# A count on VectorE in two steps: marks of half of the columns, then comparison of the other half with the marks added and summed

## The chip, the cores and the metric

The kernel runs on one core of one Trainium2 chip. The metric is the device time of one execution in microseconds; the kernel before took 3424.11 us as the median of three runs (3422.59 to 3427.55).

The core has five engines with one instruction queue each, and each queue is worked off in order: TensorE (PE in the rows, with its weight loads as PEld), VectorE (DVE), ScalarE (ACT), GpSimd (POOL) and SyncE (SP), which issues the DMAs here. They wait for each other by semaphores.

## The reference

One decoder block over a sequence of 2048 positions with 1024 features, in float32: a root-mean-square norm, one input projection, then a state-space branch and an attention branch side by side, merged with sigmoid gates, and a dense SwiGLU feed-forward layer (2816 wide).

The change lies in the attention branch. For each query an index score over all visible keys is formed, and only the 256 keys with the best scores take part in the attention:

```
rel    = relu(einsum('bqhd,bsd->bqhs', qi, ki))
iscore = einsum('bqhs,bqh->bqs', rel, wi * w_scale)
iscore = where(key_pos <= pos_q, iscore, -inf)
_, idx = top_k(iscore, 256)          # ties: the earlier key
logits = q . k[idx] * a_scale;  p = softmax(logits);  o = p . v[idx]
```

## The kernel before

**Tiles.** The 2048 queries are 16 tiles of 128, one query per partition. Tile i sees W = (i + 1) * 128 keys, so its scores are `S[i]`, a 128 x W tile of float32. Tiles 0 and 1 see no more than 256 keys and need no search.

**The key search (`topk`, from line 798).** For each query the 256th largest score is found bit by bit. A threshold `tr` is held for each query, and for each of 31 bits the kernel counts how many scores reach the threshold with that bit set; the next bit follows from the count (`un`, then `tr`, two very small VectorE instructions). The tiles are searched in four searches: tiles 2 and 3; 4 to 7; 8 to 11; 12 to 15. In each, the widest tiles are "wide": their counts are made by ScalarE with a sign function and a sum (`jka`). The narrow ones are counted by VectorE in `count` (line 849): tile 2 in the first search, tiles 4 and 5 in the second, 8 and 9 in the third, 12 and 13 in the fourth. The first count of every search is made on the float32 scores, wide tiles too. The next 15 bits of a narrow tile are counted on `H`, a copy of the upper halves of its scores as bfloat16 (threshold `tr`), the last 16 on `H` rewritten with the lower halves as uint16 (threshold `tf`); between the two stand the few wide instructions that rewrite `H` (`sgn`, `off`, `top`). At the end there is one more count on float32 scores for every tile (`gt`, line 951), and the marks of the selected keys are written out.

A count before is one VectorE instruction over all W columns: compare with the threshold, write the marks (0 or 1) to `jkd`, and sum them. In the trace it is a `TENSOR_SCALAR_CACHE_REDUCE` followed by a `DVE_READ_ACCUMULATOR`, which writes the sum out.

**What sets the order.** The whole program is written by one planner, `Pace` (line 42). It holds a clock for each engine, adds a planned cost for each instruction (`note`), and at each point takes the first of three streams (state-space branch, attention, dense layers) whose next step can start. A search step is taken as soon as VectorE is planned to be at most 7 us ahead of TensorE (`idle`, `AHEAD`). The costs there decide only the order; the engines then run at their own pace. So a cheaper count in the planner's eyes moves the work of all engines against the searches.

**What runs beside the searches.** The first and second search run beside the state-space branch and the gate projections (`gps`, `gw`), the third beside the dense layers of the first block of 512 queries (block 0), whose weights are still split into a high and a low part by GpSimd, ScalarE and VectorE (`ww<-raw`, `wd<-raw`), the fourth beside block 1 and the start of block 2. In a block TensorE writes to PSUM banks (`f`: three, and four more that the search leaves free), and VectorE empties them: `x<-f,x` adds a bank of the down projection, `g<-g,f` scales a gate, `t<-t,f` joins gate and up projection, after which ScalarE casts the result (`at<-t`) and VectorE subtracts (`at<-t,at`); only then can TensorE go on with the down projection (`f<-wd,at`).

Of the kernel before, what the change touches and what calls it, by code (L numbers as in the profile page):

```python
# [18 lines left out]
ALU = mybir.AluOpType  # L19
# [32 lines left out]
class Pace:  # L52
# [95 lines left out]
    def at(self, eng, *what):  # L148

        return lambda: self.when(eng, what) + (None,)  # L150
# [5 lines left out]
    def idle(self, eng, *what, on=None):  # L156

        return lambda: self.when(eng, what) + (on or eng,)
# [207 lines left out]
class Block:  # L366
# [431 lines left out]
    def topk(self, st, groups, KL):  # L798

        nc, at, idle = self.nc, self.pace.at, self.pace.idle  # L800
# [5 lines left out]
        def iscore(i, S, kis):  # L806
            W = (i + 1) * 128
            qi = qp.tile([128, IH, 128], F32R, name="qi")
            nc.sync.dma_start(qi.bitcast(F32), self.qi_d[i])
            for c in range(0, W, 512):  # L810
                n = min(512, W - c)
                m = min(512, (n + 255) // 256 * 256)
                for hp in range(IH // 2):
                    yield idle("PE", qi, kis, psp.free_at("tps"), on="DVE")
                    ps = psp.tile([128, 2, 512], F32, name="tps")
                    for h2 in range(2):
                        for p in range(2):
                            nc.tensor.matmul(ps[:, h2, :m], qi[:, hp * 2 + h2], kis[:, p, c:c + m],
                                             start=p == 0, stop=p == 1)
                    R = qp.tile([128, 2, 512], F32, name="R")  # L820
                    nc.scalar.activation(R[:, :, :n], ps[:, :, :n], AF.Relu)
                    for h2 in range(2):
                        w = self.wi[:, i, hp * 2 + h2:hp * 2 + h2 + 1]
                        if hp == 0 and h2 == 0:
                            nc.vector.tensor_scalar(S[:, c:c + n], R[:, 0, :n], w, None, op0=ALU.mult)
                        else:
                            nc.vector.scalar_tensor_tensor(S[:, c:c + n], R[:, h2, :n], w, S[:, c:c + n],
                                                           op0=ALU.mult, op1=ALU.add)
            dg = S[:, W - 128:W]
            nc.gpsimd.affine_select(dg, dg, pattern=[[-1, 128]], compare_op=ALU.is_ge, fill=LOW, base=0,  # L830
                                    channel_multiplier=1)
# [4 lines left out]
        S = {}  # L836
# [9 lines left out]
        self.spare_banks = 4  # L846
        jka, jkd = (qp.tile([128, L], BF16, name=n, tag="R") for n in ("jka", "jkd"))

        def count(x, i, t, c):

            nc.vector.tensor_scalar(jkd[:, :(i + 1) * 128], x, t, 0.0, op0=ALU.is_ge, op1=ALU.add, accum_out=c)

        def search(j, tiles, b, wide):

# [9 lines left out]
            for q, i in enumerate(tiles):  # L864
                yield idle("DVE")
                count(S[i], i, t[:, q:q + 1], cnt[:, q:q + 1])
# [8 lines left out]
            def missed(out, value, signs):  # L875

                if signs:
                    W = (tiles[0] + 1) * 128
                    nc.vector.tensor_scalar(out, cnt, float(W - 2 * TOPK + 1), float(value), op0=ALU.is_gt, op1=ALU.mult)
                else:  # L880
                    nc.vector.tensor_scalar(out, cnt, float(TOPK), float(value), op0=ALU.is_lt, op1=ALU.mult)

            for bit in range(30, -1, -1):
# [33 lines left out]
                for q, i in enumerate(tiles):  # L917
                    if wide:
                        nc.scalar.activation(jka[:, :(i + 1) * 128], S[i], AF.Sign, bias=t[:, q:q + 1], scale=-1.0,
                                             accum_out=cnt[:, q:q + 1])  # L920
                    else:
                        yield idle("DVE")
                        count(X[i], i, (tf if low else t)[:, q:q + 1], cnt[:, q:q + 1])
# [14 lines left out]
        for j, (tiles, b) in enumerate(states):  # L938
            n = len(tiles)
            tr = qp.tile([128, n], I32, name="trf")  # L940
            gt = qp.tile([128, n], F32, name="gt")
            fx = qp.tile([128, n], I32, name="fx")
            sg = qp.tile([128, n], I32, name="sg")
            sg2 = qp.tile([128, n], F32, name="sg2")
            ss = qp.tile([128, n], F32, name="ssum")
            nT = qp.tile([128, n], F32, name="nT")
            bf = b.bitcast(F32)
            yield idle("DVE")
            for q, i in enumerate(tiles):
                W = (i + 1) * 128  # L950
                nc.vector.tensor_scalar(jkd[:, :W], S[i], bf[:, q:q + 1], 0.0, op0=ALU.is_gt, op1=ALU.add,
                                        accum_out=gt[:, q:q + 1])
            nc.vector.tensor_scalar(fx, gt, float(TOPK), None, op0=ALU.is_ge)
            nc.vector.tensor_scalar(sg2, b, 0.0, None, op0=ALU.is_ge)
            nc.vector.tensor_scalar(sg, sg2, 2.0, -1.0, op0=ALU.mult, op1=ALU.add)
            nc.vector.tensor_tensor(tr, b, sg, op=ALU.add)
            nc.vector.copy_predicated(b, fx, tr)
            nc.vector.tensor_scalar(nT, bf, -1.0, None, op0=ALU.mult)

            todo = deque(enumerate(tiles))  # L960
            halves = deque()

            def sign():
                nonlocal order
                if todo:
                    q, i = todo.popleft()
                    W = (i + 1) * 128
                    sv, ev = (fin[:, order % 2, z, :W] for z in range(2))
                    order += 1
                    nc.scalar.activation(sv, S[i], AF.Sign, bias=nT[:, q:q + 1], scale=1.0,  # L970
                                         accum_out=ss[:, q:q + 1])
                    halves.append((q, i, W, sv, ev))
            yield idle("ACT", nT)
            sign()
            while halves:
                q, i, W, sv, ev = halves.popleft()
                yield idle("DVE", ss)
                sign()
                nc.vector.tensor_scalar(ev, sv, 0.0, None, op0=ALU.is_equal)
                nc.vector.tensor_tensor_scan(S[i], ones.to_broadcast([128, W]), ev, 0.0, op0=ALU.mult, op1=ALU.add)  # L980
                yield idle("DVE")
                r = qp.tile([128, 1], F32, name="r")
                r2 = qp.tile([128, 1], F32, name="r2")
                nc.vector.tensor_scalar(r2, gt[:, q:q + 1], -1.0, float(TOPK), op0=ALU.mult, op1=ALU.add)
                nc.vector.scalar_tensor_tensor(r, ss[:, q:q + 1], float(W - TOPK), gt[:, q:q + 1],
                                               op0=ALU.add, op1=ALU.subtract)
                nc.vector.tensor_scalar(r, r, -1.0, None, op0=ALU.mult)
                nc.vector.copy_predicated(r2, fx[:, q:q + 1], r)
                nc.vector.scalar_tensor_tensor(ev, S[i], r2, ev, op0=ALU.is_gt, op1=ALU.mult)
                yield idle("DVE")  # L990
                nc.vector.tensor_tensor(ev, ev, sv, op=ALU.subtract)
                nc.vector.tensor_scalar(ev, ev, 0.0, -BIG, op0=ALU.max, op1=ALU.mult)
                yield at("SP", ev)
                nc.sync.dma_start(self.bias_d[i], ev)
# [1008 lines left out]
```

## Time and profile before

| | |
|---|---|
| median of three runs | 3424.11 us |
| the profiled execution's own time | 3425.84 us |
| its span (first to last instruction) | 3424.1 us |
| TensorE busy | 3179.7 us, 93% |
| VectorE busy | 2150.5 us, 63% |
| ScalarE busy | 1262.8 us, 37% |
| GpSimd busy | 638.6 us, 19% |
| mean granted TensorE clock | 0.971 |

Busy times are sums over the whole span. The searches lie at about 388 to 475 us, 880 to 942, 1408 to 1640 and 2123 to 2390; what counts there is read from each stretch by itself. All instructions of the program have the same line in the profile (a recording helper), so they are told apart by the names of their tiles.

### The profile page before, as it was taken

Reading aid. Unit: us, or ns where it says so; the run is one execution under the profiler, and the core shown is the slowest. Engines: PE = TensorE matmul, PEld = TensorE weight load, DVE = VectorE, ACT = ScalarE, POOL = GpSimd, SP = SyncE. Lnnn points to the kernel's source line nnn. Section 1 sums busy time; section 2 is a strip of 40 time slices with the busy share of each in tenths; the row PEclk is TensorE's granted clock in tenths of the full one; section 3 lists DMA queues with packets and bytes.
Section 4 is the critical chain, followed back from the end, with each engine's and each line's share of the span. In section 5 each row is a group of like instructions: output and inputs, shape, how many; then the busy total and the mean of one; then the engine's idle time right before and its main releaser. Section 6 shows DMA issues by size and latency. Waiting matters only on the chain. (4 is left out here: it accounts for less than half of the span.)

```text
span 3424.1 us, 43974 instructions
## 1 busy us (share of the span) xinstructions
PE 3179.7 (93%) x16292; PEld 2684.6 (78%) x16292; DVE 2150.5 (63%) x4299; ACT 1262.8 (37%) x2192; POOL 638.6 (19%) x631
## 2 busy tenths in 40 slices
PE   6999989898978999987899999989899999999999
PEld 5889768677757887775788887768788888798887
DVE  5565686665886666889777667987766664322222
ACT  3141545454732444463024444761234342010000
POOL 3323676521222212343100000001000000000000
PEclk8999999999999999998999999989999999999999
DMA  4834433445368656566762334456453333755544
GB/s 134 250 114 117 127 106 108 157 121 156 108 222 289 225 179 226 198 239 249 262 225 112 140 108 171 165 209 227 183 187 131 115 110 141 302 207 200 205 165 183
DMA packets 321527, 605.68 MB, mean 177 GB/s; under 512 B 52896, under 2 KB 205216, under 8 KB 290592
## 3 DMA queue, kind: packets, MB, share of 16 engines
q1 hardware_dynamic: 321312, 602.86, 50.3%
q8 instruction: 129, 2.11, 0.2%
q14 instruction: 86, 0.70, 0.1%
HBM read 434.71 MB, written 166.89 MB: 176 GB/s over the span
## 5 line engine op out<-in xcount | busy, mean ns | idle before, releaser
L206 PE MATMUL f<-h,ww 128*128 128x512 f32 (+1 forms) x4416 | 1011.6, 383 | 3.9 <-DVE x L206 2.2
L206 PEld LDWEIGHTS f<-h,ww 128*128 128x128 f32 x4416 | 800.1, 190 | 160.1 <-POOL ww L206 3.4
L206 PE MATMUL f<-wd,at 128*128 128x512 f32 x2112 | 529.5, 402 | 63.9 <-ACT at L206 34.9
L206 PEld LDWEIGHTS f<-wd,at 128*128 128x128 f32 x2112 | 402.3, 194 | 160.0 <-ACT at L206 27.9
L206 PE MATMUL gps<-hT,gw 128*128 128x512 f32 x1536 | 383.6, 400 | 11.2 <-ACT gsg L206 10.0
L206 ACT ACTIVATE jka<-S,tr 128x1024 bf16<-128x1024 f32 (+6 forms) x217 | 305.8, 1409 | 181.5 <-DVE tr L206 135.8
L206 PEld LDWEIGHTS gps<-hT,gw 128*128 128x128 f32 x1536 | 285.3, 191 | 75.2 <-ACT gsg L206 12.1
L206 DVE TENSOR_TENSOR x<-f,x 128x512 f32<-128x512 f32 x352 | 237.3, 687 | 90.9 <-PE f L206 90.2
L206 DVE SCALAR_TENSOR_TENSOR t<-t,f 128x512 f32<-128x512 f32 (+1 forms) x124 | 82.4, 664 | 329.8 <-PE f L206 285.0
L206 PE MATMUL mm<-w,hT 128*128 128x512 f32 (+1 forms) x1152 | 282.0, 402 | 7.5 <-DVE hT L206 7.3
L206 PEld LDWEIGHTS mm<-w,hT 128*128 128x128 f32 x1152 | 242.1, 241 | 32.9 <-DVE hT L206 9.0
L206 DVE TENSOR_TENSOR tl<-pt,th 128x512 fp32r<-128x512 f32 (+1 forms) x288 | 184.2, 659 | 133.3 <-ACT th L206 132.0
L206 ACT CAST th<-pt 128x512 fp32r<-128x512 f32 (+1 forms) x288 | 155.9, 563 | 233.7 <-PE pt L206 231.7
L206 PE MATMUL f<-act,ww 128*128 128x512 f32 x768 | 189.8, 409 | 29.1 <-DMA act<-act 8.8
L206 POOL TENSOR_TENSOR g<-g,g 128x512 f32<-128x512 f32 x31 | 40.0, 1291 | 916.8 <-issue 553.1
L206 PE MATMUL f<-ww,mg 128*128 128x256 f32 x1536 | 193.5, 288 | 17.5 <-DMA ww<-wc 6.7
L206 PEld LDWEIGHTS f<-ww,mg 128*128 128x128 f32 x1536 | 190.3, 196 | 19.8 <-issue 7.7
L206 PEld LDWEIGHTS f<-act,ww 128*128 128x128 f32 x768 | 150.9, 199 | 67.9 <-issue 10.9
L206 ACT ACTIVATE P<-P,m 128x1024 f32<-128x1024 f32 (+7 forms) x192 | 172.2, 900 | 69.2 <-DVE m L206 68.8
L206 PE MATMUL lg<-kk,q 128*128 128x512 f32 (+1 forms) x640 | 183.9, 389 | 3.4 <-DMA kk<-kk 2.8
L206 ACT ACTIVATE t<-f 128x512 f32<-128x512 f32 (+1 forms) x92 | 53.0, 576 | 332.0 <-PE f L206 331.9
L206 ACT CAST at<-t 128x512 fp32r<-128x512 f32 (+1 forms) x92 | 55.3, 601 | 324.9 <-DVE t L206 324.9
(355 smaller groups left out, 4512.4 us busy)
## 6 DMA issues: line engine op xcount, KB each, us to landing
ww<-wc SPq DMA_DIRECT2D x180, 1024.0 KB, 5.0
wd<-wc SPq DMA_DIRECT2D x66, 1024.0 KB, 8.3
wc<-ww SPq DMA_DIRECT2D x60, 1024.0 KB, 7.8
raw<-in_w_in_dram SPq DMA_DIRECT2D x104, 256.0 KB, 3.4
wc<-wd SPq DMA_DIRECT2D x22, 1024.0 KB, 7.4
x<-in_x_dram SPq DMA_DIRECT2D x32, 512.0 KB, 5.5
gate<-gsg SPq DMA_DIRECT2D x64, 256.0 KB, 2.2
g<-gate SPq DMA_DIRECT2D x64, 256.0 KB, 5.2
```

The costliest lines, as they stand in the source:

```text
L206: return f(*args, **kw)
```

## The change

`count` becomes two instructions. With h = W / 2, the first compares the first h columns with the threshold and writes their marks to `jkd`, without a sum. The second compares the other h columns, adds the first half's marks to the results column by column, writes that to `jkd`, and sums it: the same count. The count at the end (`gt`) uses the same function.

```
-        def count(x, i, t, c):
-
-            nc.vector.tensor_scalar(jkd[:, :(i + 1) * 128], x, t, 0.0, op0=ALU.is_ge, op1=ALU.add, accum_out=c)
+        def count(x, i, t, c, op=ALU.is_ge):
+
+            h = (i + 1) * 64
+            nc.vector.tensor_scalar(jkd[:, :h], x[:, :h], t, None, op0=op)
+            nc.vector.scalar_tensor_tensor(jkd[:, h:2 * h], x[:, h:], t, jkd[:, :h], op0=op, op1=ALU.add, accum_out=c)
...
             for q, i in enumerate(tiles):
-                W = (i + 1) * 128
-                nc.vector.tensor_scalar(jkd[:, :W], S[i], bf[:, q:q + 1], 0.0, op0=ALU.is_gt, op1=ALU.add,
-                                        accum_out=gt[:, q:q + 1])
+                count(S[i], i, bf[:, q:q + 1], gt[:, q:q + 1], ALU.is_gt)
```

The planner prices the first instruction by its rule for VectorE without a sum (a quarter of the column price on 16-bit tiles, half on float32) and the second at the full column price, so its order changes everywhere behind the first search.

VectorE's queue in the fourth search, bfloat16 half, before (`un` and `tr` with the numbers 19035/19034 and 19043/19042 are the small steps of the wide tiles 15 and 14, 19051/19050 those of the narrow pair; `H_19110` and `H_19118` are tiles 12 and 13; `x_14636` is the block's output):

```order
L206 TENSOR_SCALAR jkd,cnt_19047<-H_19118,tr_19050 128x1792
L206 TENSOR_SCALAR un_19051<-cnt_19047 128x2
L206 SCALAR_TENSOR_TENSOR tr_19050<-un_19051,tr_19050 128x2
L206 SCALAR_TENSOR_TENSOR t<-t,f 128x512
L206 TENSOR_TENSOR at<-t,at 128x512
L206 TENSOR_TENSOR x_14636<-f,x_14636 128x512 x3
L206 TENSOR_SCALAR un_19035<-cnt_19031 128x1
L206 SCALAR_TENSOR_TENSOR tr_19034<-un_19035,tr_19034 128x1
L206 TENSOR_TENSOR x_14636<-f,x_14636 128x512
L206 TENSOR_SCALAR un_19043<-cnt_19039 128x1
L206 SCALAR_TENSOR_TENSOR tr_19042<-un_19043,tr_19042 128x1
L206 TENSOR_SCALAR jkd,cnt_19047<-H_19110,tr_19050 128x1664
```

The same place now (`H_19469` and `H_19478` are tiles 12 and 13):

```order
L206 TENSOR_SCALAR jkd<-H_19469,tr_19417 128x832
L206 SCALAR_TENSOR_TENSOR jkd,cnt_19414<-H_19469,tr_19417,jkd 128x832
L206 TENSOR_SCALAR jkd<-H_19478,tr_19417 128x896
L206 SCALAR_TENSOR_TENSOR jkd,cnt_19414<-H_19478,tr_19417,jkd 128x896
L206 TENSOR_SCALAR un_19418<-cnt_19414 128x2
L206 SCALAR_TENSOR_TENSOR tr_19417<-un_19418,tr_19417 128x2
L206 TENSOR_SCALAR un_19397<-cnt_19393 128x1
L206 SCALAR_TENSOR_TENSOR tr_19396<-un_19397,tr_19396 128x1
L206 TENSOR_SCALAR un_19406<-cnt_19402 128x1
L206 SCALAR_TENSOR_TENSOR tr_19405<-un_19406,tr_19405 128x1
```

Each count is two rows of half the width, the second naming `jkd` as an input. Between the first and the last count of this half VectorE's queue held 29 counts, 22 adds `x<-f,x`, 6 pairs `t<-t,f` and `at<-t,at` and 48 small pairs before; it holds 29 full and one half count, 24 adds, 7 pairs and 52 small pairs now.

VectorE's queue in the fourth search, between the two halves, before:

```order
L206 TENSOR_SCALAR H_19110<-S_18789,sgn_19788,off_19789 128x1664
L206 SCALAR_TENSOR_TENSOR H_19110<-S_18789,b_19027,H_19110 128x1664
L206 TENSOR_SCALAR un_19035<-cnt_19031 128x1
L206 SCALAR_TENSOR_TENSOR tr_19034<-un_19035,tr_19034 128x1
L206 TENSOR_SCALAR jkd<-S_18789,top_19052 128x1664
L206 TENSOR_TENSOR H_19110<-H_19110,jkd 128x1664
L206 TENSOR_SCALAR un_19043<-cnt_19039 128x1
L206 SCALAR_TENSOR_TENSOR tr_19042<-un_19043,tr_19042 128x1
L206 TENSOR_SCALAR H_19118<-S_18908,sgn_19788,off_19789 128x1792
```

The same place now (`g_20391`, `g_20393` and `g_20395` are gates of block 2):

```order
L206 TENSOR_SCALAR H_19469<-S_19151,sgn_20285,off_20286 128x1664
L206 SCALAR_TENSOR_TENSOR H_19469<-S_19151,b_19389,H_19469 128x1664
L206 TENSOR_TENSOR x_14733<-f,x_14733 128x512 x4
L206 TENSOR_SCALAR un_19397<-cnt_19393 128x1
L206 SCALAR_TENSOR_TENSOR tr_19396<-un_19397,tr_19396 128x1
L206 TENSOR_SCALAR un_19406<-cnt_19402 128x1
L206 SCALAR_TENSOR_TENSOR tr_19405<-un_19406,tr_19405 128x1
L206 TENSOR_TENSOR x_14733<-f,x_14733 128x512 x4
L206 SCALAR_TENSOR_TENSOR g_20391<-g_20391,f 128x512
L206 SCALAR_TENSOR_TENSOR g_20393<-g_20393,f 128x512
L206 SCALAR_TENSOR_TENSOR g_20395<-g_20395,f 128x512
```

The end of block 1 (its last adds) and the gates of block 2 stood beside the second half of the fourth search before; they stand between the halves now. In the third search the splits of weights by VectorE (`wd<-raw,wd` and `ww<-raw,ww`) that stand inside the search fall from 15 to 4, and the weights that are still to be split there fall from some 28 to about 20.

## Rows read from the trace of the kernel before

**Rows 1.** The page: busy times and granted clock over the whole span.
```profile
PE 3179.7 (93%) x16292; PEld 2684.6 (78%) x16292; DVE 2150.5 (63%) x4299; ACT 1262.8 (37%) x2192; POOL 638.6 (19%) x631
...
PEclk8999999999999999998999999989999999999999
```

**Rows 2.** Windows: start:end, length, busy and count per engine, clock, DMA.
```profile
380.00:480.00 100.00, 89.92 (x430) 68.92 (x428) 85.72 (x260) 55.12 (x124) 67.58 (x117) 1.00 0.28 83
880.00:942.00 62.00, 56.67 (x240) 45.73 (x240) 58.40 (x190) 50.02 (x87) 17.86 (x16) 0.97 0.30 86
1433.00:1583.00 150.00, 130.40 (x536) 104.02 (x535) 132.92 (x247) 90.02 (x116) 72.73 (x35) 0.94 0.67 231
2136.00:2233.00 97.00, 89.47 (x377) 72.17 (x376) 89.12 (x187) 75.26 (x80) 0.00 (x0) 0.96 0.42 159
2233.00:2390.00 157.00, 137.14 (x706) 117.05 (x705) 123.85 (x227) 60.84 (x66) 10.32 (x8) 0.93 0.63 233
```

**Rows 3.** Waits of TensorE, 2136 to 2390 us: total us, times, longest.
```profile
PE f L206 <- ACT at L206: 9.1, 1, 9.1
PE f L206 <- DVE t L206: 7.1, 4, 2.4
PE f L206 <- DVE x L206: 6.8, 4, 4.5
```

**Rows 4.** VectorE's timeline, fourth search: start, duration in us, instruction.
```profile
2206.24 2.08 DVE L206 TENSOR_SCALAR_CACHE_REDUCE jkd<-H,tr 128x1792 bf16<-128x1792 bf16 x1
2208.24 0.09 DVE L206 DVE_READ_ACCUMULATOR jkd<-H,tr 128x1 f32 x1
2208.36 0.17 DVE L206 TENSOR_SCALAR un<-cnt 128x2 int32<-128x2 f32 x1
2208.57 0.16 DVE L206 SCALAR_TENSOR_TENSOR tr<-un,tr 128x2 int32<-128x2 int32 x1
```

**Rows 5.** Groups by form, the counts: busy us, mean ns | idle before.
```profile
L206 DVE TENSOR_SCALAR_CACHE_REDUCE jkd<-H,tr 128x1792 bf16<-128x1792 bf16 x15 | 31.1, 2076 | 0.2
L206 DVE TENSOR_SCALAR_CACHE_REDUCE jkd<-H,tr 128x1664 bf16<-128x1664 bf16 x15 | 29.1, 1940 | 0.0
L206 DVE TENSOR_SCALAR_CACHE_REDUCE jkd<-H,tr 128x1280 bf16<-128x1280 bf16 x15 | 23.1, 1539 | 0.1
L206 DVE TENSOR_SCALAR_CACHE_REDUCE jkd<-H,tr 128x1152 bf16<-128x1152 bf16 x15 | 21.1, 1404 | 0.1
...
L206 DVE TENSOR_SCALAR_CACHE_REDUCE jkd<-H,tr 128x384 bf16<-128x384 bf16 x15 | 9.0, 602 | 0.0
```

**Rows 6.** Groups by form, undisturbed neighbours of the two new instructions.
```profile
L206 DVE TENSOR_SCALAR fin<-fin 128x1664 bf16<-128x1664 bf16 x2 | 1.2, 594 | 1.3 <-ACT fin L206 1.3
L206 DVE TENSOR_SCALAR fin<-fin 128x896 bf16<-128x896 bf16 x2 | 0.8, 391 | 0.0
L206 DVE TENSOR_SCALAR jkd<-S,top 128x1792 uint16<-128x1792 f32 x1 | 1.1, 1148 | 0.0
L206 DVE SCALAR_TENSOR_TENSOR fin<-S,r,fin 128x896 bf16<-128x896 f32 x1 | 1.2, 1151 | 0.0
L206 DVE SCALAR_TENSOR_TENSOR fin<-S,r,fin 128x640 bf16<-128x640 f32 x1 | 0.9, 884 | 0.0
L206 DVE SCALAR_TENSOR_TENSOR fin<-S,r,fin 128x384 bf16<-128x384 f32 x1 | 0.6, 618 | 0.0
```

**Rows 7.** Groups by form, 2136 to 2233 us: dense work and small steps.
```profile
L206 DVE TENSOR_TENSOR x<-f,x 128x512 f32<-128x512 f32 x22 | 14.3, 684 | 0.0
L206 DVE SCALAR_TENSOR_TENSOR tr<-un,tr 128x1 int32<-128x1 int32 x34 | 5.4, 160 | 1.2
L206 DVE TENSOR_SCALAR un<-cnt 128x1 int32<-128x1 f32 x33 | 4.8, 147 | 0.0
L206 DVE TENSOR_TENSOR at<-t,at 128x512 fp32r<-128x512 f32 x6 | 4.2, 693 | 5.6 <-ACT at L206 5.6
```

**Rows 8.** Groups by form, third search, GpSimd at work beside VectorE.
```profile
L206 DVE SCALAR_TENSOR_TENSOR tr<-un,tr 128x1 int32<-128x1 int32 x51 | 31.8, 623 | 1.7
L206 DVE TENSOR_SCALAR jkd<-S,top 128x1280 uint16<-128x1280 f32 x1 | 3.0, 3009 | 0.0
```

## The prediction

> **What bounds the kernel now.** I read the page's busy line first [rows 1]: TensorE has work for 3179.7 of 3424.1 us, so all other engines together can give back at most the 244 us in which it idles, plus what its clock loses (the clock line dips to 0.8 in a few slices). VectorE's 63% says nothing by itself, since the counts lie in four short searches; so I cut windows there [rows 2]. In the bfloat16 half of the fourth search (2136 to 2233 us) VectorE is busy 89.1 of 97 us, TensorE 89.5, and GpSimd not at all. In the rest of that search (2233 to 2390) TensorE idles 157 − 137.1 = 19.9 us, and TensorE's waits over both stretches [rows 3] name VectorE twice (7.1 and 6.8 us) and once the cast that stands behind VectorE's join (9.1 us). In the third search's first half (1433 to 1583) VectorE is busy 132.9 of 150, TensorE idles 19.6, and GpSimd is busy 72.7. So the searches are the places where VectorE holds TensorE up, and only the fourth has VectorE to itself.
>
> **The new count, step by step.** A full-width count of 1792 columns costs 2076 ns [rows 5], and the next dependent instruction starts 0.04 us after the instruction's nominal end (2206.24 to 2208.36 is 2.12 us [rows 4]). The price per column is (2076 − 602) / 1408 = 1.047 ns: one column per step, though all operands have 16 bits. The first new instruction has its neighbour in the comparisons on 16-bit tiles without a sum: 594 ns at 1664 columns and 391 at 896 [rows 6], which is 0.264 ns a column and about 154 ns fixed. The second new instruction, an accumulating two-tensor form, doesn't occur before. Its neighbours are the two-tensor forms without a sum: 1151, 884 and 618 ns at 896, 640 and 384 columns [rows 6], 1.04 ns a column. I take these, since the sum costs the present count no extra per column. The bounds: half that column price if 16-bit operands are taken two at a time, and twice it if the sum takes a second step.
>
> The second instruction reads what the first wrote, so it starts 0.04 us after it ends, as the pair un, tr does [rows 4]; its read-out starts 0.08 us before its nominal end and costs 0.12, as now. A new count is thus first + second + 0.08 us:
> - 1792 columns: 0.391 + 1.151 + 0.08 = 1.622 against 2.116, a gain of 0.494
> - 1664 (halves of 832): 0.374 + 1.084 + 0.08 = 1.538 against 1.980, 0.442
> - 1280: 0.323 + 0.884 + 0.08 = 1.287 against 1.579, 0.292
> - 1152: 0.306 + 0.817 + 0.08 = 1.203 against 1.444, 0.241
> - 768 and 640, whose old prices lie on the same line (1.04 and 0.91 us with the gap): about 0.09 and 0.04
> - 384: 0.205 + 0.418 + 0.08 = 0.703 against 0.642, a loss of 0.061
>
> Each is made 31 times: 29.0 us of VectorE in the fourth search, 16.5 in the third, about 4 in the second, and −1.9 in the first. The 28 counts on float32 (14 tiles, one at each end) gain little: the comparison on float32 runs at 1148 ns for 1792 columns [rows 6], so at half that width about 0.68 us, and 0.68 + 1.151 + 0.08 is 0.2 us below 2.12 at this width, less for narrower tiles; some 3 us in all. Sum on VectorE alone: about 50 us. None of this is TensorE's time yet.
>
> **What it is worth in the fourth search.** The order there puts 24 adds, 7 join pairs and 52 small pairs beside the counts of the first half, where 22, 6 and 48 stood. By the durations in [rows 7] (a small pair 0.147 + 0.160, an add 14.3 / 22 = 0.65, a join pair twice 0.69) that is 1.3 + 1.4 + 1.2 = 3.9 us more, against 14.5 pairs of counts x 0.936 = 13.6 us less: VectorE needs about 79 us where it needed 89.1. TensorE gets one more projection there (48 matmuls) and two adds' worth of down projection (12), at 89.47 / 377 = 0.237 us each [rows 2] 14 us, and needs some 104. VectorE is then no longer the bound: I take 5 of the 7.5 us of TensorE's idle time there. In the second stretch 19.9 us stand idle; I take 6, because the 9.1 us wait at a block's end is a chain (VectorE, ScalarE, VectorE) that stays, even if counts in front of it get shorter. The clock is granted at 0.96 and 0.93 in these stretches [rows 2]; 0.04 x 89.5 + 0.07 x 137.1 = 13 us are lost that way, and with a good third of the idle time gone I take 3 of them. Together 14 us. Bounds: nothing, if the waits only move; 27 + 13 = 40 us, if all idle time and the whole clock loss go.
>
> **The other searches.** Here the change adds something the rows of the fourth search don't show. The small step tr<-un,tr takes 160 ns there [rows 7] and 623 ns in the third search [rows 8], 51 times: 0.463 x 51 = 23.6 us in which VectorE stood beside a busy GpSimd (35 instructions, 72.7 us). A comparison without a sum took 3009 ns at 1280 columns [rows 8], where 1148 ns do for 1792 [rows 6]. The present counts show no such stretch (1539 ns at 1280 columns, on the line of the others [rows 5]). So two-tensor forms and comparisons without a sum are held up by GpSimd, counts with a sum are not, and the change turns each of the 155 narrow counts of searches one to three into two instructions of the kind that is held up.
>
> The Trainium skill has the rule for it ("SBUF — State Buffer", section "Who interferes with whom"): a tensor_scalar in a two-port mode, but not its accumulating form, and an instruction with two SBUF inputs contend with GpSimd for a shared port pair, and the second to come waits for the whole instruction. The trace agrees: 623 against 160 ns.
>
> The upper bound of the extra hold-up is GpSimd's busy time that isn't held against VectorE yet: in the third search's first half 72.7 − 23.6 = 49 us. But one GpSimd instruction can hold up VectorE only once, and every bit's small steps already run into it (23.6 / 35 = 0.7 us of about 2.1 each). With more exposed instructions I take 1.0 each; that is 10 us there, and less with some 20 weights to split where 28 stood. It eats most of the 16.5 us, and the splits that leave VectorE's queue in that search make up the rest: I count the third search at 0. In the first (GpSimd 67.6 of 100 us in short instructions) and second (17.9 of 62) I count a loss of 2 us of TensorE's time, since gate matmuls cover most of the delay; if that cover runs out it is up to 15.
>
> **Sum.** 3425.84 (the profiled execution) − 14 + 0 + 2 = 3413.8 us. The profiled execution lies 1.7 us above the median of the runs, so in their terms 3412.
>
> **Rivals.**
> - *No change* (3417 to 3431): the waits in [rows 3] are set by how far the planner lets VectorE run ahead, 7 us whatever a count costs, and by the chain at a block's end; with cheaper counts the same waits come at other places. For it: 9.1 of 23 us are such a chain. Against it: VectorE is busy 92% of the stretch and idles only behind casts.
> - *GpSimd's hold on VectorE wins* (slower): if each GpSimd instruction beside the third search costs VectorE 1.7 us in place of 0.7, that is 35 us over the 35 in half of the search against 8 us saved, and VectorE, at 133 of 150 us, passes it on to TensorE. With the first two searches' 5 to 10 us less the fourth's 14, that gives about 3442. It decides from about 1.2 us per GpSimd instruction on. For it: the 3009 ns; against it: fewer splits in that search, and the hold-ups that are paid already.
> - *The accumulating form takes two steps a column.* Then a pair in the fourth search costs 1.80 us more than taken. Held to the 16 uint16 bits that is 28.8 us, all of the 29.0; the third search loses 4. About 3428. Against it: [rows 6] show one column per step with one float32 and one bfloat16 input from SBUF, but without a sum. The Trainium skill says this of the form ("Vector Engine (DVE) Microarchitecture Reference", section "7. Points that are easy to get wrong"): with two non-bf16 SBUF sources its throughput halves. Only one source is non-bf16 in the uint16 half, and no row here has the sum.
> - *The accumulating form takes 16-bit columns two at a time.* The second instruction falls by 0.52 ns a column, a pair in the fourth search by another 0.9 us, 28 us in all, and nearly all of TensorE's 27 us idle there goes: about 3392. Against it: the present counting form has 16-bit operands too and runs one column per step.
>
> **How the numbers follow.** Forecast (3400 to 3417) 0.50; no change 0.19; GpSimd's hold 0.17; two steps 0.08, half of it within the bound; pairs 0.06. A measurement of this kernel can tell about 0.2% from no change, 7 us. Faster by more: 0.50 + 0.06 = 0.56; within: 0.19 + 0.04 = 0.23; slower: 0.17 + 0.04 = 0.21. The range reaches from just above the pairs' case to short of the far side of GpSimd's hold: 3394 to 3436; the forecast's own is 3400 to 3417.
>
> **What would show it.** Right: the 832- and 896-column instructions near 374, 391, 1084 and 1151 ns in the fourth search; TensorE's idle time there down by 10 us or more; little change in the third. Wrong: the second instruction near 2 us or 0.65 us; the new instructions of the third search a microsecond above those prices with TensorE waiting longer; or new prices as computed, with the fourth search's idle time as large as before, which would mean that the planner's order and not VectorE's time set it.

## The result, and the profile after

The changed kernel takes 3402.05 us in the median of four runs (3396.26 to 3403.34), the kernel before 3425.83 us in the runs beside it. The ratio is 0.9925 (95% interval 0.9907 to 0.9944): 24 us faster where 12 were forecast. The time lies in the forecast's range (3400 to 3417), 2 us above its lower end. That was partly luck: two terms of the sum were wrong in opposite directions, as the experiments show. The profiled execution took 3402.73 us.

The page after, busy times and granted clock, answers to [rows 1]:

```profile
PE 3177.4 (93%) x16292; PEld 2685.5 (79%) x16292; DVE 2124.6 (62%) x4530; ACT 1273.6 (37%) x2207; POOL 650.5 (19%) x632
...
PEclk8999999999989999998999999999999999999999
```

VectorE lost 2150.5 − 2124.6 = 26 us of work, not the 50 of the prediction, while TensorE's idle time (span less busy) fell from 244.4 to 3400.6 − 3177.4 = 223.2 us. To see where, I cut both executions at the first count of the fourth search: start:end, length, busy time and count of each engine, then clock, DMA share and GB/s. Before:

```profile
0.00:2123.50 2123.50, 1932.53 (x9934) 1629.40 (x9935) 1461.86 (x3023) 893.65 (x1632) 611.39 (x606) 0.96 0.52 173
2123.50:3424.07 1300.57, 1247.17 (x6359) 1055.24 (x6357) 688.68 (x1277) 369.17 (x560) 27.22 (x25) 0.98 0.49 184
```

After:

```profile
0.00:2165.30 2165.30, 1972.24 (x10078) 1664.11 (x10079) 1472.79 (x3196) 908.42 (x1651) 622.72 (x607) 0.96 0.51 172
2165.30:3400.60 1235.30, 1205.19 (x6215) 1021.39 (x6213) 651.82 (x1335) 365.22 (x556) 27.73 (x25) 0.99 0.51 188
```

Below, the stretch up to that count is "the head" and the rest "the tail". The new order has 144 matmuls more in the head, so lengths are compared only between kernels with one order. Idle time of TensorE (length less busy) is 191.0 us in the head and 53.4 in the tail before, 193.1 and 30.1 after: the whole gain is in the tail. TensorE's busy time in the tail falls by 42.0 us, but most of that is work moved into the head: 96 matmuls `f<-h,ww` and 48 `f<-wd,at`, which cost 0.235 and 0.243 us each in the tail before, 34.2 us together:

```profile
L206 PE MATMUL f<-h,ww 128*128 128x512 f32 x2435 | 572.4, 390 | 0.0
L206 PE MATMUL f<-wd,at 128*128 128x512 f32 x1296 | 315.1, 396 | 20.1 <-ACT at L206 10.7 <-DVE t L206 7.1 <-DVE x L206 2.3
```

The other 8 us go with the granted clock, which rises from 0.98 to 0.99 there. So the tail gave 23 us of idle time and some 8 us of matmuls that cost less. The head took part of it back: 2 us of idle time, and 39.7 us more busy time for the 34 us of work that came into it.

The counts of the fourth search after, by form (busy us, mean ns | idle before):

```profile
L206 DVE SCALAR_TENSOR_TENSOR jkd<-H,tf,jkd 128x896 bf16<-128x896 uint16 x16 | 18.4, 1151 | 0.6
...
L206 DVE SCALAR_TENSOR_TENSOR jkd<-H,tr,jkd 128x832 bf16<-128x832 bf16 x15 | 16.3, 1085 | 0.5
L206 DVE SCALAR_TENSOR_TENSOR tr<-un,tr 128x1 int32<-128x1 int32 x62 | 9.9, 159 | 2.1
...
L206 DVE TENSOR_SCALAR jkd<-H,tr 128x896 bf16<-128x896 bf16 x15 | 6.7, 450 | 0.3
L206 DVE TENSOR_SCALAR jkd<-H,tr 128x832 bf16<-128x832 bf16 x15 | 6.4, 430 | 0.0
```

The second step is what [rows 6] gave, to within a nanosecond: 1151 and 1085 for 1151 and 1084, on uint16 as on bfloat16. The first step is 56 to 59 ns dearer than its neighbour (430 and 450 for 374 and 391). The small step stands at 159 ns as in [rows 7]: nothing holds VectorE up here. The same steps over the whole kernel, where GpSimd works beside them in the second and third search (384 columns: second, 576: third; 704 is a float32 count of the third):

```profile
L206 DVE SCALAR_TENSOR_TENSOR jkd<-H,tr,jkd 128x576 bf16<-128x576 bf16 x15 | 19.9, 1327 | 0.5
...
L206 DVE SCALAR_TENSOR_TENSOR jkd<-H,tf,jkd 128x384 bf16<-128x384 uint16 x16 | 14.5, 907 | 0.6
...
L206 DVE SCALAR_TENSOR_TENSOR jkd<-H,tf,jkd 128x576 bf16<-128x576 uint16 x16 | 13.1, 818 | 0.6
L206 DVE TENSOR_SCALAR jkd<-H,tf 128x384 bf16<-128x384 uint16 x16 | 12.0, 751 | 0.4
...
L206 DVE TENSOR_SCALAR jkd<-H,tr 128x384 bf16<-128x384 bf16 x15 | 4.8, 318 | 0.3
...
L206 DVE SCALAR_TENSOR_TENSOR jkd<-S,tr,jkd 128x704 bf16<-128x704 f32 x1 | 2.9, 2897 | 0.1
```

One form has two prices: 818 ns at 576 columns in the uint16 half of the third search and 1327 in its bfloat16 half; 318 and 751 for a first step of 384 in the two halves of the second. GpSimd (the fifth busy time) worked 69.7 of 140 us beside the dear half of the third search and 10.3 of 90 beside the other:

```profile
1475.00:1615.00 140.00, 115.76 (x455) 92.11 (x454) 129.35 (x249) 78.79 (x101) 69.71 (x30) 0.90 0.57 201
1630.00:1720.00 90.00, 78.48 (x402) 66.71 (x401) 59.35 (x149) 30.25 (x40) 10.29 (x8) 0.94 0.84 312
```

That is the hold-up the prediction argued from [rows 8], now on the counts themselves.

TensorE's waits in the fourth search and just behind it after, 2165 to 2480 us (total us, times, longest); [rows 3] end at 2390:

```profile
PE f L206 <- DVE ss L206: 7.1, 1, 7.1
...
PE f L206 <- DVE x L206: 2.7, 2, 1.4
...
PE f L206 <- ACT at L206: 1.3, 1, 1.3
```

The 9.1 us behind the cast (`at`) are 1.3 now, the 6.8 behind the adds (`x`) 2.7, and the join (`t`, 7.1) is gone from the list. What is left longest is a wait at a block's start, for the norm (`ss`). It isn't new; it stood behind the stretch of [rows 3] (2123 to 2480 us before):

```profile
PE f L206 <- DVE ss L206: 7.4, 1, 7.4
```

### The profile page after: what moved, and what is told of

Its sections match the earlier page's. It is cut to its first block, busy times and chain, and to the rows that moved or that the text cites. A ratio compares the mean times of both kernels' runs of the same rounds, so it can differ in the third digit from the quotient of the medians.

```text
span 3400.6 us, 44225 instructions
## 1 busy us (share of the span) xinstructions
PE 3177.4 (93%) x16292; PEld 2685.5 (79%) x16292; DVE 2124.6 (62%) x4530; ACT 1273.6 (37%) x2207; POOL 650.5 (19%) x632
## 5 line engine op out<-in xcount | busy, mean ns | idle before, releaser
L206 ACT ACTIVATE jka<-S,tr 128x1536 bf16<-128x1536 f32 (+6 forms) x217 | 305.6, 1408 | 198.3 <-DVE tr L206 125.1
```

The source lines that it names most:

```text
L206: return f(*args, **kw)
```

## The experiments

Two things change at once: what a count costs on VectorE, and the order that the planner writes when a count has another price. That price went up, not down. `note` takes half of the column price off a `tensor_scalar` on 16-bit tiles even when it sums (`short` lets operands one column wide pass for 16-bit):

```
    RATE = {"DVE": (1.05e-3, 0.07), "ACT": (0.84e-3, 0.06), "POOL": (2.25e-3, 0.07)}
...
            elif eng == "DVE" and op in ("tensor_scalar", "tensor_tensor") and short:
                cost -= size * r / 2
            if "accum_out" in kw:
                cost += 0.2 if eng == "ACT" else 0.14
```

So an old count of 1792 columns was planned at 1792 x 0.00105 / 2 + 0.07 + 0.14 = 1.15 us, and it takes 2.12. The two steps are planned at 0.305 + 1.151 us and 0.15 between them, for a result that the next instruction reads: 1.61 us, and they take 1.68. For the planner the change makes a count dearer and, by accident, nearly true.

Theory A: VectorE's shorter counts in the fourth search give the gain. Theory B, its rival: the order gives it, whatever a count costs. The function `count` can be taken apart, because the planner's `note` (the price) and the instruction emitted through `eng` are separate calls. All queues of a pair with "the same order" are then equal instruction for instruction, the counts themselves excepted. Each ratio is to the kernel before as it ran beside that kernel (medians 3424.22, 3427.18 and 3428.09 us in three groups of runs).

### The new order with the old counts

```
             note("DVE", "tensor_scalar", (jkd[:, :h], x[:, :h], t, None), ...)
             note("DVE", "scalar_tensor_tensor", (jkd[:, h:2 * h], x[:, h:], t, jkd[:, :h]), ...)
+            v.eng.tensor_scalar(jkd[:, :2 * h], x, t, 0.0, op0=op, op1=ALU.add, accum_out=c)
```

> Every engine's queue stands exactly as in the changed kernel, but each count is the old single instruction. Theory A (the gain is VectorE time in the fourth search): the queue there is 29 us longer than in the changed kernel with the same work planned beside it, so TensorE waits for it; 20 to 35 us slower than the changed kernel, at 3420 to 3440 us. Rival B (the gain comes from the new order, whatever a count costs): within 8 us of the changed kernel, 3394 to 3410 us.

Measured: 3391.61 us, ratio 0.9896 (0.988 to 0.9913). That is below both ranges. Without a single cheaper count the kernel is some 10 us faster than the changed one (the two intervals just overlap, the single runs don't). So B holds in part, and over the whole kernel the two-step counts lose. Head and tail, to be read against those of after (same matmul counts):

```profile
0.00:2139.70 2139.70, 1967.08 (x10078) 1663.88 (x10079) 1451.35 (x3021) 908.77 (x1651) 615.92 (x607) 0.96 0.52 174
2139.70:3387.17 1247.47, 1204.33 (x6215) 1021.15 (x6213) 680.74 (x1265) 365.63 (x556) 27.22 (x25) 0.99 0.50 186
```

In one order, two steps in place of one cost 2165.3 − 2139.7 = 25.6 us in the head and save 1247.5 − 1235.3 = 12.2 in the tail. VectorE's own work: +21.4 us in the head (1472.79 − 1451.35), −28.9 in the tail (651.82 − 680.74).

### The old order with the new counts

```
             note("DVE", "tensor_scalar", (jkd[:, :2 * h], x, t, 0.0), dict(op0=op, op1=ALU.add, accum_out=c))
+            v.eng.tensor_scalar(jkd[:, :h], x[:, :h], t, None, op0=op)
+            v.eng.scalar_tensor_tensor(jkd[:, h:2 * h], x[:, h:], t, jkd[:, :h], op0=op, op1=ALU.add, accum_out=c)
```

> Every engine's queue stands exactly as in the kernel before, but each count is the two new instructions. Theory A: TensorE's 42 us of idle time from 2123 to 2480 us fall by 15 to 25 us, since VectorE is ahead of its old order; 3400 to 3415 us, the third search within 5 us of before. Rival B: the waits stand where the order puts them; 3418 to 3430 us.

Measured: 3416.66 us, ratio 0.9977 (0.9964 to 0.9989), between the two ranges.

```profile
0.00:2139.30 2139.30, 1945.13 (x9934) 1639.27 (x9935) 1476.70 (x3198) 893.34 (x1632) 617.04 (x606) 0.96 0.51 172
2139.30:3411.63 1272.33, 1240.25 (x6360) 1052.29 (x6358) 659.16 (x1347) 367.75 (x560) 27.74 (x25) 0.99 0.50 188
```

Against before (one order): the head is 15.8 us longer with 14.8 us more VectorE work, the tail 28.3 us shorter with 29.5 less; TensorE's idle time in the tail falls from 53.4 to 32.1. So A holds in the fourth search in its own right, and the loss in the head is there in either order. Only 3.2 of the 15.8 us are idle time of TensorE; 12.6 are busy time, 1945.13 us for the 9934 matmuls that took 1932.53 before. So the loss comes mainly as dearer matmuls here; in the new order it comes mainly as idle time (193.1 us in place of 172.6).

### Two steps in the fourth search alone, and in the first three alone

```
+            if i >= 12:      # the second kernel: i < 12
                 nc.vector.tensor_scalar(jkd[:, :h], x[:, :h], t, None, op0=op)
                 nc.vector.scalar_tensor_tensor(jkd[:, h:2 * h], x[:, h:], t, jkd[:, :h], ...)
+            else:
+                nc.vector.tensor_scalar(jkd[:, :2 * h], x, t, 0.0, op0=op, op1=ALU.add, accum_out=c)
```

> Two steps in the fourth search only (tiles 12 to 15), old counts before it. Theory A: the whole gain stays and the 8 us by which block 0 started later are won back; 3390 to 3402 us. Rival B or a gain spread over all searches: 3405 to 3425 us.

> Two steps in the first three searches only, old counts in the fourth. Theory A: no gain, the hold-up by GpSimd shows as a small loss; 3422 to 3436 us. A gain spread over all searches: 3405 to 3418 us.

Measured: 3392.19 us, ratio 0.9899 (0.9883 to 0.9915), and 3432.09 us, ratio 1.0017 (1.0008 to 1.0026), both where theory A had them. The two add up: −1.01% and +0.17% make −0.84%, and the whole change has −0.75%. In microseconds the fourth search gives 35 and the first three take 6. Fourth alone:

```profile
0.00:2125.40 2125.40, 1928.38 (x9934) 1627.90 (x9935) 1464.51 (x3023) 893.76 (x1632) 609.55 (x606) 0.97 0.52 173
2125.40:3385.56 1260.16, 1237.54 (x6360) 1049.64 (x6358) 659.38 (x1347) 367.50 (x560) 27.75 (x25) 0.99 0.51 189
```

### The order of that kernel with the old counts

```
+            if i < 12: v.tensor_scalar(jkd[:, :2 * h], x, t, 0.0, ...); return
             note(...first step...); note(...second step...)
+            v.eng.tensor_scalar(jkd[:, :2 * h], x, t, 0.0, op0=op, op1=ALU.add, accum_out=c)
```

> The queues stand as in the kernel with two steps in the fourth search only, but every count is the old single instruction. Theory G (of that kernel's 32 us the order gives some 18 and the cheaper counts some 14): 3400 to 3412 us, TensorE idle near 28 us in the fourth search. Rival H (the gain needs the cheaper counts): 3418 to 3430 us, idle near 42 us.

Measured: 3404.22 us, ratio 0.9928 (0.9915 to 0.994), as theory G had it.

```profile
0.00:2119.20 2119.20, 1932.07 (x9935) 1628.29 (x9936) 1461.43 (x3023) 893.37 (x1632) 612.30 (x606) 0.97 0.52 173
2119.20:3396.65 1277.45, 1239.16 (x6359) 1050.55 (x6357) 688.10 (x1277) 367.95 (x560) 27.19 (x25) 0.99 0.50 187
```

Now the fourth search has all four corners (the one with the counts alone is the kernel in the old order, whose first three searches have two steps too). Tail: 1300.6 us with neither, 1277.5 with the order alone (−23.1), 1272.3 with the counts alone (−28.3), 1260.2 with both (−40.4). TensorE's idle time there: 53.4, 38.3, 32.1, 22.6. Each alone removes much of the same waits, so they don't add. By the ratios of all runs the order gives 0.72% and the counts on top of it 0.29%, 10 us. The waits in 2123 to 2490 us show how. The 9.1 us behind the cast (`at`) are 6.9 with the counts alone and 5.3 with the order alone; only both together take it to 0.8. And the order alone lets a wait come back at the block's start (`ss`), 7.4 us before and 13.9 now. Counts alone, then order alone:

```profile
PE f L206 <- ACT at L206: 6.9, 1, 6.9
...
PE f L206 <- DVE ss L206: 1.6, 1, 1.6
```

```profile
PE f L206 <- DVE ss L206: 13.9, 1, 13.9
PE f L206 <- ACT at L206: 5.3, 1, 5.3
```

### The new order, two steps only where GpSimd is idle

```
             note(...first step...); note(...second step...)
+            if i >= 12: v.eng.tensor_scalar(...); v.eng.scalar_tensor_tensor(...)
+            else: v.eng.tensor_scalar(jkd[:, :2 * h], x, t, 0.0, op0=op, op1=ALU.add, accum_out=c)
```

> The queues stand as in the changed kernel; the two steps are executed for tiles 12 to 15 only, the other counts are the old instruction. Theory C (the order and the instructions are two effects that add: the order is worth some 30 us, the cheaper counts 12 more in the fourth search, and the two steps cost 20 or more in searches one to three where GpSimd holds them up): TensorE's idle time up to the end of block 0 as in the run with the new order and old counts (155 us), in the fourth search below 20 us; 3370 to 3385 us. Rival D (the gains overlap, the fourth search's idle time goes only once): 3388 to 3398 us.

Measured: 3378.15 us, ratio 0.9866 (0.9849 to 0.9884). It beats both kernels: 49 us below before and, by the two ratios, 20 below the changed one, as theory C had it. Against the new order with old counts throughout (0.9896) the gain of 0.3% is not clear of noise.

```profile
0.00:2145.70 2145.70, 1971.18 (x10078) 1664.45 (x10079) 1453.95 (x3021) 908.57 (x1651) 614.67 (x607) 0.96 0.52 174
2145.70:3383.26 1237.56, 1204.59 (x6216) 1020.42 (x6214) 651.81 (x1335) 365.13 (x556) 27.78 (x25) 0.99 0.50 188
```

It differs from after only in how 155 of its counts in the first three searches, and the float32 ones beside them, are made: 0.59% of the time, 20 us. Its head idles 174.5 us where after's idles 193.1.

### Other prices for the planner

If a lower planned price were good by itself (theory E), the old counts with a lower price would gain too. Theory E took the price of the two steps for the lower one, some 70% of the old; by `note` it is 1.61 us to 1.15, so its two kernels test the other direction. And if the gain of the fourth search hung on one lucky order (against which theory J says that it holds as long as the planned price is no lower than the true one), a planned price off by 0.2 us would lose it. Five kernels:

```
+            w = int(W * 0.85)      # the second kernel: 0.55; both emit the old count over all W columns
+            self.pace.note("DVE", "tensor_scalar", (jkd[:, :w], x[:, :w], t, 0.0), ...)
...
+            self.pace.free["DVE"] += 0.2      # two steps in all four searches
...
+            self.pace.free["DVE"] += 0.2      # two steps in the fourth search alone; the last kernel: -0.2
+            self.pace.done[self.pace.key(jkd[:, :h])] = (self.pace.free["DVE"] + 0.15, "DVE")
```

> Old counts, but the planner prices each as if it had 85% of its columns. Theory E (a lower planned price of a count helps by itself, because fewer small steps stand in front of the join instructions that TensorE waits for): about half of the order's gain, 3400 to 3415 us. Rival F (which order comes out is chance): anywhere from 3385 to 3440 us, without relation to the price.

> Old counts, planned at 55% of their columns, which is below the price that the change plans (about 70% for the widest tile). Theory E: at least the order's gain, 3375 to 3395 us, or a turn where VectorE falls behind its plan. Rival F: no relation to the price, 3385 to 3440 us.

> The two steps everywhere, as in the changed kernel, but planned 0.2 us dearer, which is about what they cost on the chip. Theory E: some of the order's gain is lost, 3404 to 3420 us. Rival F: no relation, 3385 to 3430 us. A third reading, that a truer price makes a better order: 3380 to 3395 us.

> Two steps in the fourth search only, planned 0.2 us dearer each, so that another order comes out there. Theory J (the fourth search gains in any order planned near the true price, since VectorE has 29 us less to do there): 3385 to 3402 us. Rival K (the order that came out is a lucky one): above 3405 us.

> Two steps in the fourth search only, planned 0.2 us cheaper each. Theory J: a little worse than at the true price, since VectorE then falls some 12 us behind its plan over the 62 counts; 3392 to 3408 us. Rival K: no relation, 3385 to 3430 us.

Measured: old counts at 85% of their price 3452.06 us, ratio 1.0069 (1.0057 to 1.0082); at 55% 3487.34, 1.0177 (1.0164 to 1.019). Both lie above rival F's range too (3385 to 3440). Theory E falls: too low a price costs 24 and 61 us. Two steps everywhere, planned 0.2 us dearer: 3402.59, 0.9934 (0.9922 to 0.9946), not to be told from after; but this edit, without the line on `done`, lets the 0.2 us run beside the 0.15 that the second step waits anyway, so the plan is only 0.05 us dearer and the kernel tests little. Fourth search alone, 0.2 us dearer: 3387.72, 0.9886 (0.9871 to 0.9902), not to be told from the same without it (0.9899). 0.2 us cheaper: 3403.77, 0.9927 (0.9915 to 0.994), 10 us lost. So J holds here. With the planned price of a count of 1792 columns beside what it takes, ten kernels read one way:

| counts | takes | planned, and the ratio |
|---|---|---|
| old | 2.12 us | 0.73: 1.0177; 1.01: 1.0069; 1.15: 1 (before); 1.61: 0.9896 |
| two steps | 1.68 us | 1.15: 0.9977; 1.61: 0.9925 (after); 1.66: 0.9934 |
| two steps in the fourth search alone | 1.68 us there | 1.41: 0.9927; 1.61: 0.9899; 1.81: 0.9886 |

The further the plan lies below what a count takes, the slower the kernel; a price 0.13 us too high costs nothing. At 1.15 us in place of 2.12, and in proportion for the narrower tile, VectorE falls some 58 us behind its plan over the 62 counts of the fourth search. That this is what TensorE then waits for is argued, not shown. Chance (rivals F and K) would hardly give three rows in one direction. The old count planned at its full 2.12 us was not run. Old counts at 85%, head and tail:

```profile
0.00:2124.50 2124.50, 1913.19 (x9791) 1613.68 (x9792) 1447.11 (x3018) 895.68 (x1638) 591.28 (x590) 0.95 0.51 170
2124.50:3457.30 1332.80, 1278.53 (x6503) 1079.80 (x6501) 696.63 (x1290) 371.33 (x564) 27.21 (x25) 0.99 0.49 184
```

By the same time as before, TensorE has done 9791 matmuls where it had done 9934: its idle time in the head is 211.3 us (191.0 before). The loss lies ahead of the fourth search.

### The two kinds of count, with and without GpSimd beside them

A piece ahead of the kernel before, on tiles of its own: 12 old counts (line 1999) and 12 new ones (lines 2002 and 2003) of 1792 columns with GpSimd idle, then the same beside 30 GpSimd subtractions (line 2011). It ran once.

```
+        for f in (old, new):
+            for _ in range(12): f()
+        nc.gpsimd.tensor_tensor(pa, pa, mc[:, :1].to_broadcast([128, 1024]), op=ALU.add)
+        for _ in range(30): nc.gpsimd.tensor_tensor(pb, pa, pb, op=ALU.subtract)
+        for f in (old, new):
+            for _ in range(12): f()
```

> The kernel before with a piece ahead of it that the reference doesn't need: 12 old counts of 1792 bfloat16 columns and 12 new ones with GpSimd idle, then the same beside 30 subtractions of 128x1024 on GpSimd (2.4 us each). If only comparisons without a sum and two-tensor forms are held up by GpSimd: old count 2.08 us in both parts; first step 0.45 and second 1.15 us alone, and beside GpSimd the two steps together 2 us or more longer. If the hold-up seen in the searches has another cause: the same durations in both parts.

Measured, VectorE's groups by form: GpSimd idle (the first three rows), and beside it, where GpSimd is at work throughout (50 to 75.9 us, and 77.3 to 130.2):

```profile
L1999 DVE TENSOR_SCALAR_CACHE_REDUCE mk<-mx,mt 128x1792 bf16<-128x1792 bf16 x12 | 24.9, 2079 | 0.4
...
L2003 DVE SCALAR_TENSOR_TENSOR mk<-mx,mt,mk 128x896 bf16<-128x896 bf16 x12 | 13.8, 1151 | 0.4
L2002 DVE TENSOR_SCALAR mk<-mx,mt 128x896 bf16<-128x896 bf16 x12 | 5.4, 453 | 0.4
...
L1999 DVE TENSOR_SCALAR_CACHE_REDUCE mk<-mx,mt 128x1792 bf16<-128x1792 bf16 x12 | 24.9, 2079 | 2.5 <-POOL pa L2009 2.1
...
L2003 DVE SCALAR_TENSOR_TENSOR mk<-mx,mt,mk 128x896 bf16<-128x896 bf16 x10 | 31.1, 3107 | 0.4
L2002 DVE TENSOR_SCALAR mk<-mx,mt 128x896 bf16<-128x896 bf16 x9 | 21.6, 2403 | 0.3
```

GpSimd's groups in the two stretches beside old (50 to 75.9 us) and new counts (75.9 to 130.2):

```profile
L2011 POOL TENSOR_TENSOR pb<-pa,pb 128x1024 f32<-128x1024 f32 x11 | 25.7, 2339 | 0.9
...
L2011 POOL TENSOR_TENSOR pb<-pa,pb 128x1024 f32<-128x1024 f32 x20 | 53.6, 2680 | 1.6
```

The old count takes 2079 ns either way. Each step of the new one takes 1.95 us more (2403 − 453, 3107 − 1151), and GpSimd's own instructions are longer too (2680 for 2339 ns). Per count, start of first step to start of the next (VectorE's timeline):

```profile
80.48 2.40 DVE L2002 TENSOR_SCALAR mk<-mx,mt 128x896 bf16<-128x896 bf16 x1
82.92 3.11 DVE L2003 SCALAR_TENSOR_TENSOR mk<-mx,mt,mk 128x896 bf16<-128x896 bf16 x1
85.96 0.08 DVE L2003 DVE_READ_ACCUMULATOR mk<-mx,mt,mk 128x1 f32 x1
86.07 2.40 DVE L2002 TENSOR_SCALAR mk<-mx,mt 128x896 bf16<-128x896 bf16 x1
```

That is 5.59 us beside a GpSimd that never rests, against some 2.12 for an old count and 0.45 + 1.15 + 0.08 = 1.68 for a new one without GpSimd. This fits the Trainium skill ("SBUF — State Buffer", section "Who interferes with whom"): whoever comes second to the shared port pair waits for the other's whole instruction. That the one-input count with a sum is free of it, and that a sum does not free the two-input form, this run shows directly.

## Why the prediction was right or wrong, step by step

- **What bounds the kernel: right.** VectorE held TensorE up in the fourth search, where GpSimd is idle; 29 us less VectorE work there, in an unchanged order, shortened the tail by 28, of which 21 are idle time of TensorE and 7 are matmuls that cost less.
- **The price of the new count: right but for 0.06 us.** The second step is exact. The first is 56 to 59 ns dearer than the neighbour taken for it. On 62 counts that is 3.6 us. Savings on VectorE in the fourth search: 29.0 predicted from the bit counts alone, 28.9 and 29.5 measured with the float32 counts included.
- **The fourth search, −14 us: mis-sized; this is the larger error.** It gave 35 us. The step that failed is "I take 6, because the 9.1 us wait at a block's end is a chain … that stays, even if counts in front of it get shorter": the wait fell to 1.3 us. By shorter counts alone it falls only to 6.9, so the chain does stay for the most part; what took the rest is the new order, which this step left out. The waits for VectorE itself were sized too small as well: with the counts alone the one for the join (7.1) goes altogether and the one for the norm behind the search falls from 7.4 to 1.6. In all 23 us of idle time went where 11 were taken (5 + 6), and matmuls that cost less gave some 8 us where 3 were taken for the clock. The upper bound of the term, 40 us, was the better estimate.
- **The third search 0, the first two +2: mis-sized the other way.** The mechanism was right and its size too small. In an unchanged order the two steps lengthen the head by 15.8 us (by 25.6 in the new order), while VectorE's work there grows by 14.8 (21.4) us instead of falling by 16.5 + 4 − 1.9 = 18.6. The change's new order gives part of that back, so that the first three searches cost 6 us net.
- **The rule that one GpSimd instruction holds VectorE up only once** was part of that working, and the separate counts beside GpSimd agree with it: 20 subtractions held up 20 steps. But each new step meets an instruction of its own, so a count is held up twice, and each time by 1.95 us where 1.0 us for each GpSimd instruction was taken. That is beside a GpSimd that never rests; in the searches it rests part of the time.
- **The rivals.** *GpSimd's hold wins*: its mechanism is real, its price (35 − 8 = 27 us in the third search, 5 to 10 in the others) was somewhat above the 16 to 26 us that the counts by themselves cost, but it didn't decide, since the fourth search gave more than twice the 14 us set against it. *No change*: with both effects the waits did not come back elsewhere, but its mechanism is there, since the order alone made the wait at the block's start 6.5 us longer. *Two steps a column* and *pairs*: both fall by one row, 1151 ns at 896 columns. The rule that the Trainium skill gives ("Vector Engine (DVE) Microarchitecture Reference", section "7. Points that are easy to get wrong") isn't contradicted for the form with a sum: one of its two inputs is always bfloat16 here, and no run has a sum with two that aren't. Without a sum two float32 inputs show no halving: 1281 ns at 1024 columns before (`hh<-x,rr,gB`), on the price line of [rows 6].
- **The order, which the prediction weighed only by its counts of instructions,** was worth 23 us in the fourth search by itself. It changed because the planner's price of a count rose towards what a count takes, not because counts got cheaper; nothing in the prediction weighs that. Its section on what would be wrong had asked for the planner's order as a cause only if the idle time stayed; it fell for both reasons.

Left open: by which waits a truer price makes the better order. Only the orders' worth is measured (0.72% for the fourth search's alone, 1.04% for all), and that it follows the planned price. That the pointer operand is what makes the first step dearer than its neighbour, which compares with a constant, was not tried.

## What to carry to other kernels

Splitting one summed VectorE instruction into a short unsummed one and a two-input one paid here only where GpSimd is idle; price both forms beside a busy GpSimd before using them everywhere, and choose by place. Where a planner orders the program by prices, compare them with the trace first: here a count was planned at about half of what it takes, and an order written at a truer price was worth 0.7 to 1% without any cheaper instruction. There a changed instruction is two changes: run the new order with the old instruction, and the old order with the new one, before crediting either. And a wait that ends a chain behind the shortened work should be given both its ends, nothing and its whole length.

## What the runs showed of the hardware that was not expected

- A two-input comparison with a sum is held up by GpSimd (1151 to 3107 ns), though the one-input form with a sum is not (2079 ns in both cases). Both sides pay: the GpSimd subtractions rose from 2339 to 2680 ns.
- In the kernel the hold-up partly moves rather than adds. The small steps of the wide tiles, in one order, took 88.4 us with the old counts and 77.1 with the new:

```profile
L206 DVE SCALAR_TENSOR_TENSOR tr<-un,tr 128x1 int32<-128x1 int32 x232 | 88.4, 381 | 8.0
```

```profile
L206 DVE SCALAR_TENSOR_TENSOR tr<-un,tr 128x1 int32<-128x1 int32 x232 | 77.1, 332 | 7.9
```

(the first row is of the new order with old counts, the second of after): 11 us less beside GpSimd. In the old order it is 81.8 us with the old counts and 73.9 with the new. That GpSimd meets a count first is the likely reason, not shown.
- A comparison on 16-bit columns with a threshold for each query costs 450 ns at 896 columns where the neighbour in [rows 6] has 391; the difference is mostly a fixed one (56 ns at 832 columns by the same line, 59 at 896).
